# Two up-product chunks as products over halves of the rows, in a two-layer encoder on one core

## The chip, the core and the metric

The kernel runs on one core of a Trainium2 chip. The core's engines are TensorE (PE in the profile, with its weight loads as PEld), VectorE (DVE), ScalarE (ACT), GpSimd (POOL) and SyncE (SP), which here only issues transfers. The metric is device time in microseconds (us) of one execution. Each number is from runs on the chip or from the hardware profile of one execution.

## The reference

The program is a trunk of two encoder layers over 256 tokens of width 2048 (`D_MODEL`), in float32. Each layer is a norm, a token mixer and a residual add, then a norm, a gated MLP with a convolution of width 3 and a residual add. Layer 0 mixes with a bidirectional mLSTM, layer 1 with a bidirectional HGRN2. The change lies in the MLP of layer 0:

```python
D_FF = 5504
def conv_glu(hn, w_up, conv_w, conv_b, w_down):
    u = hn @ w_up
    a, v = jnp.split(u, 2, axis=-1)
    ...
    c = conv_b
    for j in range(CONV_W):
        c = c + ap[:, j:j + s] * conv_w[j]
    return (jax.nn.gelu(c, approximate=False) * v) @ w_down
```

## The kernel before, in words

**Products in two parts.** Every large product is made of float32r products. A weight piece `raw` is cast by ScalarE to `wh` (line 154), and VectorE subtracts that from `raw` to get the rest `wl` (line 155). The activations are split in the same way: `xt` holds, for each block of 128 features, 256 columns (tokens) of the leading part and 256 of the rest. One product of `wh` with all 512 columns (line 202) and one of `wl` with the first 256 (line 206) make up a 128x128 block of weights against all tokens.

**Chunks and pieces.** All weights go through one stream. `split_weights` (line 123) loads them in transfers of 1 MB, casts and subtracts them in pieces of 1024 columns, with three `raw` buffers and four each of `wh` and `wl`. `stream` (line 161) asks for pieces three ahead and walks over the chunks. An up-chunk (kind "fm", 256 output features) has sixteen blocks of input features (`nk`, index k) in four pieces. For each k it has two feature blocks f, gate (f = 0) and value (f = 1), each with its own PSUM bank `ps[f]`, and for each f the products "h" and "l". That is 64 products per chunk.

**Eviction.** At the end of a chunk `done_up` (line 842) empties the banks: `fm_scaled` has ScalarE copy columns 256 to 511 of a bank to `b` (line 231), VectorE add columns 0 to 255 (line 232) and multiply by the norm's factor (line 237). Then VectorE makes the convolution (lines 851 to 853), ScalarE the Gelu (line 854), VectorE the gating (line 855), and the result is split for the down-product (lines 857, 858).

**Banks.** The pool `psm` has four banks under the tag "mm". A chunk takes two of them (line 175), so one chunk can be evicted while the next one is multiplied.

**Order.** The program is written in the order of the loops, and a scheduler places the instructions on each engine's queue by its own simulated times. [...]

**The MLP's chunks.** `ffn` (loop at line 862) has two parts: 22 up-chunks and then their four down-chunks, and 21 up-chunks and their four down-chunks. In the trace the up-chunks of the first part of layer 0 follow each other every 11.09 us; their Gelu (line 854) starts at 548.30 us for i = 12, at 559.39 for i = 13 and at 570.49 for i = 14.

Of the kernel before, what the change touches and what calls it, by code (L numbers as in the profile page):

```python
# [8 lines left out]
F32 = mybir.dt.float32  # L9
# [3 lines left out]
ALU = mybir.AluOpType  # L13
PSUM = bass.MemoryType.PSUM

P = 128
T = 256
# [38 lines left out]
def trunk_kernel(ctx, tc, xT, x_d, fg_d, pp_d, cst_d, w_first, w_aq, w_ak, w_av, w_ao, w_aout,  # L56
                 w_bq, w_bv, w_bg, w_bout, w_up, w_down, out, mscr):
    nc = tc.nc
    act, dve, pool, pe = nc.scalar, nc.vector, nc.gpsimd, nc.tensor
# [3 lines left out]
    ev = ctx.enter_context(tc.tile_pool(name="ev", bufs=1))  # L63
    psm = ctx.enter_context(tc.tile_pool(name="psm", bufs=4, space=PSUM))
# [13 lines left out]
    def col(name, i):  # L78
        o = OFF[name] + i
        return pp[:, o:o + 1]  # L80
# [5 lines left out]
    class Side:  # L86
        def __init__(self):
            self.now, self.jobs = 0.0, []
# [25 lines left out]
    side = Side()  # L114


    class Chunk:
        def __init__(self, kind, src, nk, x, done, before=None, last=False, swap=()):
            self.last, self.swap = last, swap
            self.kind, self.src, self.nk, self.x, self.done, self.before = kind, src, nk, x, done, before  # L120
            self.width = {"fm": 256, "tm": 512, "first": 512 + P}[kind]

# [38 lines left out]
    def stream(chunks):  # L161
        pieces = split_weights(chunks)
        ready = []

        def fetch():
            p = next(pieces, None)
            if p is not None:
                ready.append(p)

        for _ in range(LOOK):  # L170
            fetch()
        for ch in chunks:
            if ch.before:
                ch.before()
            ps = [psm.tile([P, 512], F32, tag="mm", name="mm") for _ in range(3 if ch.kind == "first" else 2)]
            k = 0
            while k < ch.nk:
                fetch()
                wh, wl, n = ready.pop(0)
                if ch.last and k + sum(p[2] for p in ready) + n == ch.nk:  # L180
                    pieces_, k0 = [(wh, wl, n)] + ready, k
                    for t in range(2):
                        k = k0
                        for wh, wl, n in pieces_:
                            for kk in range(n):
                                x, c = ch.x(k), slice(kk * 512, (kk + 1) * 512)
                                xh, xl = x[:, t * P:(t + 1) * P], x[:, T + t * P:T + (t + 1) * P]
                                pe.matmul(ps[t], xh, wh[:, c], start=False, stop=False)
                                pe.matmul(ps[t], xh, wl[:, c], start=False, stop=False)
                                pe.matmul(ps[t], xl, wh[:, c], start=False, stop=k == ch.nk - 1)  # L190
                                k += 1
                        ch.half(ps[t], t)
                    return
                if ch.kind == "fm":
                    ops = [(kk, f, part) for kk in range(n) for f in range(2) for part in "hl"]
                    for i in ch.swap if k == 0 else ():
                        ops[2 * i + 1:2 * i + 3] = ops[2 * i + 2], ops[2 * i + 1]
                    for kk, f, part in ops:
                        x = ch.x(k + kk)
                        c = kk * ch.width + f * P  # L200
                        if part == "h":
                            pe.matmul(ps[f], wh[:, c:c + P], x, start=k + kk == 0, stop=False)  # L202
                            continue
                        if f:
                            side.tick(0.65)
                        pe.matmul(ps[f][:, 0:T], wl[:, c:c + P], x[:, 0:T], start=False, stop=k + kk == ch.nk - 1)  # L206
                    k += n
                    continue
                for kk in range(n):
                    x = ch.x(k)  # L210
                    st, sp = k == 0, k == ch.nk - 1
                    c = slice(kk * 512, (kk + 1) * 512)
                    for t in range(2):
                        xh, xl = x[:, t * P:(t + 1) * P], x[:, T + t * P:T + (t + 1) * P]
                        pe.matmul(ps[t], xh, wh[:, c], start=st, stop=False)  # L215
                        pe.matmul(ps[t], xh, wl[:, c], start=False, stop=False)  # L216
                        pe.matmul(ps[t], xl, wh[:, c], start=False, stop=sp)  # L217
                    if ch.kind == "first":
                        pe.matmul(ps[2], wh[:, 512:512 + P], x, start=st, stop=False)
                        pe.matmul(ps[2][:, 0:T], wl[:, 512:512 + P], x[:, 0:T], start=False, stop=sp)  # L220
                    side.tick(1.3)
                    k += 1
            ch.done(ps)

    def split(dst, src, gcol, pin=lambda ins: ins):
# [8 lines left out]
    def fm_scaled(ps, R, dst, scale=None):  # L234
        fm_sum(ps, dst)
        if scale is None:
            dve.tensor_tensor(dst, dst, R, ALU.mult)
        else:
            dve.scalar_tensor_tensor(dst, dst, scale, R, ALU.mult, ALU.mult)
# [144 lines left out]
    def project(wsrc, nk, x, norm):  # L384

        def done(c):
            def f_(ps):
                for t in range(2):
                    h = hm[:, t, 512 * c:512 * c + 512]
                    dve.tensor_tensor(h, h, ps[t], ALU.add)  # L390
                if norm is not None:
                    norm.add(c)
            return f_
        chunks = [Chunk("tm", wsrc(c), nk, x, done(c)) for c in range(4)]
        if isinstance(norm, FinalNorm):
            chunks[3].last, chunks[3].half = True, norm.half
        return chunks

    def slot(j, name, more=None):
        where = keep if j < KT else more  # L400
        return where.tile([P, 2 * T], F32R, tag=f"yt{j}", name=f"{name}{j}")
# [429 lines left out]
    def ffn(layer, norm, nxt):  # L831
        stack = ExitStack()
        box = {}
        chunks = []

        def begin():
            box["mp"] = stack.enter_context(tc.tile_pool(name="ff", bufs=1))
            box["mp"].tile([P, LEAD], F32, name="lead")
            if isinstance(nxt, FinalNorm):
                nxt.begin(box["mp"])  # L840

        def done_up(f, i, GT):
            def go(ps):
                mp, R = box["mp"], norm.R
                a = mp.tile([P, T], F32, tag="a", bufs=2, name="a")
                v = mp.tile([P, T], F32, tag="v", bufs=2, name="v")
                c = mp.tile([P, T], F32, tag="c", bufs=2, name="c")
                fm_scaled(ps[0], R, a)
                fm_scaled(ps[1], R, v)
                cw = [col("conv_w", (layer * 3 + w) * FT + f) for w in range(3)]  # L850
                dve.tensor_scalar(c, a, cw[1], col("conv_b", layer * FT + f), ALU.mult, ALU.add)
                dve.scalar_tensor_tensor(c[:, 1:T], a[:, 0:T - 1], cw[0], c[:, 1:T], ALU.mult, ALU.add)
                dve.scalar_tensor_tensor(c[:, 0:T - 1], a[:, 1:T], cw[2], c[:, 0:T - 1], ALU.mult, ALU.add)
                act.activation(c, c, AF.Gelu)
                dve.tensor_tensor(c, c, v, ALU.mult)
                g = slot(i, "g", mp)
                act.copy(g[:, 0:T], c)
                dve.tensor_tensor(g[:, T:2 * T], c, g[:, 0:T].bitcast(F32), ALU.subtract)
                GT.append(g)
            return go  # L860

        for part, (f0, nf) in enumerate(((0, FA), (FA, FB))):
            GT = []
            for i in range(nf):
                chunks.append(Chunk("fm", w_up[layer, f0 + i], KT, norm.x, done_up(f0 + i, i, GT),
                                    begin if f0 + i == 0 else None,
                                    swap=(1 + (layer == 0),) if part and i == 0 else ()))
            chunks += project(lambda c: w_down[layer, c][:, f0 * 512:(f0 + nf) * 512], nf,
                              lambda k, GT=GT: GT[k], nxt if part else None)
        return chunks, stack.close  # L870
# [7 lines left out]
    for i in range(39):  # L878
        o = i % 4 * QUAD
        pe.matmul(idle[o:o + QUAD, 0:120], ones[:, 0:QUAD], ones[:, 0:120], start=True, stop=True)  # L880
    n0, n1, n2, n3 = Norm("mix_g", 0), Norm("ffn_g", 0), Norm("mix_g", KT), Norm("ffn_g", KT)
    nf = FinalNorm()
    chunks = mlstm(n0, n1)
    c, close0 = ffn(0, n1, n2)
    chunks += c
    c = hgrn(n2, n3)
    b = c[0].before
# [6 lines left out]
    c, close1 = ffn(1, n3, nf)  # L894
    chunks += c
    stream(chunks)
    close1()

# [81 lines left out]
```

## Time and profile before

| | |
|---|---|
| time, median of 3 runs | 2419.44 us (2418.76 to 2421.82) |
| the profiled execution: time | 2421.37 us |
| the profiled execution: span of the core | 2419.6 us |
| granted TensorE clock, mean | 0.999 |
| PE busy | 2406.7 us, 99% of the span |
| products of line 202 (512 columns) | 3776, 1315.6 us busy |
| products of line 206 (256 columns) | 3776, 1048.8 us busy |
| VectorE, ScalarE busy | 1694.1 us (70%), 1221.1 us (50%) |

The time of the profiled execution lies 1.9 us above the median of the runs, and its span 1.8 us below its own time. In the profile's rows a line gives its line number in the kernel, the engine, the operation, output and inputs by name, the shapes, and how often it occurs; `128*32` ahead of the shapes stands for the rows and columns of the array that a product uses. Products overlap in the array, so the sum of their durations is more than the time they take; starts tell the pace.

### The profile page before, as it was taken

The numbers are of one execution on the slowest core, as the hardware profiler recorded it, in microseconds if no ns is written. First come the engines' busy times: TensorE is split into PE (matmuls) and PEld (weight loads), VectorE is DVE, ScalarE is ACT, GpSimd is POOL, SyncE is SP. The second block draws the span as 40 slices with busy tenths as digits, with TensorE's granted clock in tenths as the row PEclk, the third lists the DMA queues.
The fourth block names the chain that finished last, engine by engine and source line by source line (L and its number), as shares of the span: only waits on it lengthen the run. The fifth ranks groups of instructions, "written<-read, shape, count | busy, mean of one in ns | idle before, by whom it ended". The sixth has DMA issues, their size and how long they took to land.

```text
span 2419.6 us, 36956 instructions
## 1 busy us (share of the span) xinstructions
PE 2406.7 (99%) x14646; PEld 2060.3 (85%) x14646; DVE 1694.1 (70%) x2784; ACT 1221.1 (50%) x1879; POOL 161.7 (7%) x223
## 2 busy tenths in 40 slices
PE   9999999999999999999999999999999999999998
PEld 7888888888888888888888888888888888888887
DVE  7766656777645777656898989885777754677754
ACT  6655455444434445445555555555544443444443
POOL 0100000000000000001222222220000000000000
PEclk9999999999999999999999999999999999999999
DMA  8654555555555555555545554555555555555554
GB/s 290 200 182 162 186 176 189 190 188 189 181 196 201 188 187 189 192 185 183 173 173 175 175 175 167 168 185 190 183 191 190 192 188 195 194 190 192 192 188 142
DMA packets 66925, 451.90 MB, mean 187 GB/s; under 512 B 7600, under 2 KB 8368, under 8 KB 14144
## 3 DMA queue, kind: packets, MB, share of 16 engines
q1 hardware_dynamic: 64656, 442.92, 54.0%
q0 software_dynamic: 1232, 5.31, 0.9%
q8 instruction: 114, 1.87, 0.3%
q10 hardware_dynamic: 864, 1.32, 0.2%
q14 instruction: 59, 0.48, 0.1%
HBM read 447.35 MB, written 2.16 MB: 186 GB/s over the span
## 4 chain that ended last, share of the span: by engine, by line
PE 98%; DMA 1%; DVE 0%; issue 0%; ACT 0%; SPq 0%; POOLq 0%; POOL 0%; DVEq 0%
PE mm L202 36%; PE mm L206 18%; PE mm L215 13%; PE mm L216 13%; PE mm L217 13%; DMA gx<-in_xT 1%; PE pn L533 1%; PE py L763 1%; PE pd L713 0%; PE pz L288 0%; PE pa L713 0%; PE S L519 0%; PE pz L784 0%; PE pa L738 0%; PE pa L737 0%
## 5 line engine op out<-in xcount | busy, mean ns | idle before, releaser
L155 DVE TENSOR_TENSOR wl<-raw,wh 128x1024 fp32r<-128x1024 f32 (+1 forms) x848 | 1031.9, 1218 | 582.3 <-ACT wh L154 572.4
L202 PE MATMUL mm<-xt,wh 128*128 128x512 f32 x3776 | 1315.6, 394 | 0.0
L154 ACT CAST wh<-raw 128x1024 fp32r<-128x1024 f32 (+1 forms) x848 | 881.2, 1041 | 859.0 <-PE mm L217 400.9
L206 PE MATMUL mm<-xt,wl 128*128 128x256 f32 x3776 | 1048.8, 278 | 0.0
L202 PEld LDWEIGHTS mm<-xt,wh 128*128 128x128 f32 x3776 | 707.0, 188 | 160.7
L206 PEld LDWEIGHTS mm<-xt,wl 128*128 128x128 f32 x3776 | 710.0, 188 | 3.2 <-DVE wl L155 0.3
L217 PE MATMUL mm<-wh,g 128*128 128x512 f32 x674 | 262.8, 390 | 0.0
L215 PE MATMUL mm<-wh,g 128*128 128x512 f32 x674 | 262.5, 390 | 0.0
L216 PE MATMUL mm<-wl,g 128*128 128x512 f32 x674 | 262.3, 389 | 0.0
L215 PE MATMUL mm<-wh,xt 128*128 128x512 f32 x512 | 198.9, 393 | 2.9 <-ACT xt L226 2.1
L216 PE MATMUL mm<-wl,xt 128*128 128x512 f32 x512 | 198.5, 392 | 0.2 <-DVE wl L155 0.2
L217 PE MATMUL mm<-wh,xt 128*128 128x512 f32 x512 | 198.0, 391 | 0.0
L231 ACT COPY b<-mm 128x256 f32<-128x256 f32 x237 | 87.6, 369 | 166.6 <-PE mm L206 166.5
L217 PEld LDWEIGHTS mm<-wh,g 128*128 128x128 f32 x674 | 126.5, 188 | 26.5
L215 PEld LDWEIGHTS mm<-wh,g 128*128 128x128 f32 x674 | 126.5, 188 | 26.4
L216 PEld LDWEIGHTS mm<-wl,g 128*128 128x128 f32 x674 | 126.5, 188 | 25.8
L215 PEld LDWEIGHTS mm<-wh,xt 128*128 128x128 f32 x512 | 95.1, 188 | 23.2 <-ACT xt L226 3.3
L217 PEld LDWEIGHTS mm<-wh,xt 128*128 128x128 f32 x512 | 96.1, 188 | 20.0 <-DVE xt L227 0.4
L216 PEld LDWEIGHTS mm<-wl,xt 128*128 128x128 f32 x512 | 96.1, 188 | 19.9 <-DVE wl L155 1.2
L232 DVE TENSOR_TENSOR a<-mm,b 128x256 f32<-128x256 f32 x86 | 36.5, 424 | 52.2 <-ACT b L231 52.2
L705 DVE COPY kq<-QK 128x256 f32<-128x256 f32 x224 | 69.6, 335 | 0.0
L731 POOL TENSOR_TENSOR G<-G 128x384 f32<-128x384 f32 (+2 forms) x96 | 67.8, 706 | 6.3
(206 smaller groups left out, 1836.7 us busy)
## 6 DMA issues: line engine op xcount, KB each, us to landing
raw<-in_w_up SPq DMA_DIRECT2D x172, 1024.0 KB, 5.0
raw<-in_w_down SPq DMA_DIRECT2D x80, 1024.0 KB, 4.8
raw<-in_w_bq SPq DMA_DIRECT2D x48, 1024.0 KB, 5.0
raw<-in_w_ao SPq DMA_DIRECT2D x16, 1024.0 KB, 4.8
raw<-in_w_aout SPq DMA_DIRECT2D x16, 1024.0 KB, 4.7
raw<-in_w_bv SPq DMA_DIRECT2D x16, 1024.0 KB, 4.7
raw<-in_w_bg SPq DMA_DIRECT2D x16, 1024.0 KB, 4.7
raw<-in_w_bout SPq DMA_DIRECT2D x16, 1024.0 KB, 4.8
```

The lines of the kernel that those rows point to most:

```text
L154: pin(act.copy(wh[:, :m], r))
L155: pin(dve.tensor_tensor(wl[:, :m], r, wh[:, :m].bitcast(F32), ALU.subtract))
L202: pe.matmul(ps[f], wh[:, c:c + P], x, start=k + kk == 0, stop=False)
L206: pe.matmul(ps[f][:, 0:T], wl[:, c:c + P], x[:, 0:T], start=False, stop=k + kk == ch.nk - 1)
L215: pe.matmul(ps[t], xh, wh[:, c], start=st, stop=False)
L216: pe.matmul(ps[t], xh, wl[:, c], start=False, stop=False)
L217: pe.matmul(ps[t], xl, wh[:, c], start=False, stop=sp)
L231: act.copy(b, ps[:, T:2 * T])
L232: dve.tensor_tensor(dst, ps[:, 0:T], b, ALU.add)
L533: pe.matmul(pn[:, 0:258], w, v, start=(i == 0), stop=(i == len(parts) - 1))
L705: dve.tensor_copy(m[:, j].rearrange("k (m p j) -> k m p j", p=2, j=h), blocks(z, h, 0, T))
L731: pool.tensor_tensor(G2, G[:, 0:6 * n:2], G[:, 1:6 * n:2], ALU.mult)
```

## The change

The chunks i = 13 and i = 14 of the first part in layer 0 get `rows=64`. Such a chunk takes four banks rather than two. Each of its products becomes two, one over rows (partitions) 0 to 63 of weights and activations and one over rows 64 to 127, the first into bank `ps[f]`, the second into `ps[2 + f]`. The columns stay as they were. At the end of the chunk ScalarE copies each of the two lower banks whole to a buffer of 512 columns, VectorE adds it to the upper bank in place, and `done_up` goes on as before. The buffer shares the tag "jk", of which there is one. All other chunks keep their code.

```diff
-        def __init__(self, kind, src, nk, x, done, before=None, last=False, swap=()):
-            self.last, self.swap = last, swap
+        def __init__(self, kind, src, nk, x, done, before=None, last=False, swap=(), rows=P):
+            self.last, self.swap, self.rows = last, swap, rows
...
-            ps = [psm.tile([P, 512], F32, tag="mm", name="mm") for _ in range(3 if ch.kind == "first" else 2)]
+            ps = [psm.tile([P, 512], F32, tag="mm", name="mm") for _ in range(3 if ch.kind == "first" else 4 if ch.rows < P else 2)]
...
+                if ch.rows < P:
+                    for kk in range(n):
+                        x = ch.x(k + kk)
+                        for f in range(2):
+                            c = kk * ch.width + f * P
+                            for w, m in ((wh, 2 * T), (wl, T)):
+                                for r in range(2):
+                                    o = slice(r * 64, r * 64 + 64)
+                                    pe.matmul(ps[2 * r + f][:, 0:m], w[o, c:c + P], x[o, 0:m],
+                                              start=m > T and k + kk == 0, stop=m == T and k + kk == ch.nk - 1)
+                        side.tick(0.65)
+                    k += n
+                    continue
...
+            if ch.rows < P:
+                for f in range(2):
+                    b = ev.tile([P, 512], F32, tag="jk", bufs=1, name="half")
+                    act.copy(b, ps[2 + f])
+                    dve.tensor_tensor(ps[f], ps[f], b, ALU.add)
             ch.done(ps)
...
-                                    swap=(1 + (layer == 0),) if part and i == 0 else ()))
+                                    swap=(1 + (layer == 0),) if part and i == 0 else (),
+                                    rows={13: 64, 14: 64}.get(i, P) if not layer and not part else P))
```

## The prediction

> **What bounds the kernel now.** I read the busy shares and the chain that ended last first, to see which engine sets the end.
>
> ```profile
> PE 2406.7 (99%) x14646; PEld 2060.3 (85%) x14646; DVE 1694.1 (70%) x2784; ACT 1221.1 (50%) x1879; POOL 161.7 (7%) x223
> ...
> PE 98%; DMA 1%; DVE 0%; issue 0%; ACT 0%; SPq 0%; POOLq 0%; POOL 0%; DVEq 0%
> ```
>
> PE is the path from end to end, so a stage costs what PE needs for it. The Gelu rows in ScalarE's timeline (line 854) put the thirteenth of the first layer's up-chunks (i = 12) at 548.30 us, so the matmuls of i = 13 and 14 lie at about 544.05 to 566.24. The windows view gives this stretch, and PE's timeline its grain:
>
> ```profile
> 544.05:555.14 11.09, 11.09 (x67) 9.69 (x65) 8.11 (x13) 5.47 (x9) 0.00 (x0) 1.00 0.58 191
> 555.14:566.24 11.10, 11.10 (x67) 9.71 (x66) 8.10 (x13) 5.49 (x9) 0.00 (x0) 1.00 0.55 190
> ```
> ```profile
> 544.04 0.39 PE L202 MATMUL mm<-xt,wh 128*128 128x512 f32 x1
> 544.27 0.27 PE L206 MATMUL mm<-xt,wl 128*128 128x256 f32 x1
> 544.39 0.40 PE L202 MATMUL mm<-xt,wh 128*128 128x512 f32 x1
> ```
>
> A chunk takes 11.09 us, with no gap. Starts, not durations, are the price: a 512-column product holds PE for 0.23 us and a 256-column one for 0.116 (544.27 to 544.39), together 0.347; 32 such pairs are the 11.1 us. Durations (394, 278 ns) add about 0.16 of fill that overlaps the next product. So the two chunks are 22.19 us, DVE has 3 us of slack in each, ScalarE 5.6.
>
> **The products.** Each of the 128 products of the two chunks becomes two, over rows 0 to 63 and 64 to 127, with the same columns: 256 products of 231 or 116 ns. Does a product over half the rows cost half? The nearest rows say no: the 64-row transpose of 64 columns takes 247 ns, the 128-row ones of 128 columns 272, and the 25 ns between them are 64 columns at the rate of the up-products (116 ns for 256). Columns set the time. One after another the 256 would therefore take 44.4 us, 22.2 more than now. They can only stay near 22 us if the two halves, which use different rows of the array, run at the same time. No row of the trace has two row groups at once. The nearest one has four column groups at once:
>
> ```profile
> L880 PEld LDWEIGHTS idle<-ones x78: 110/177/178, 1.1 to 4.5; 128*32 128x32 f32 x78
> L880 PE MATMUL idle<-ones x78: 266/407/408, 1.1 to 4.6; 128*32 128x120 f32 x78
> ```
>
> 78 products start within 3.5 us, 45 ns apart, though each lasts 407: they start in bunches of four, 7 ns apart, with about 200 ns from bunch to bunch. The hgrn products (line 713) do the same with their weight loads:
>
> ```profile
> 1165.78 0.80 PEld L713 LDWEIGHTS pd<-kq 128*32 128x32 f32 x79
> ```
>
> 79 loads of 108 ns each fit in 0.80 us. I take it that row groups overlap as column groups do. [...]
>
> **The order.** Overlap needs the two halves next to each other, since products start in order. The order of the changed program (as built) shows where the scheduler put them. In i = 13 the second feature block's banks come free late, so for the first six k its upper halves (6 of 512 columns, 6 of 256) are issued in one run and its lower halves in another: 6 × 0.347 = 2.08 us of each without a partner. In i = 14, 25 upper-half products of the first block (13 × 0.231 + 12 × 0.116 = 4.40 us) come before the first lower half, which overlaps the last of them (-0.23); later a run of five upper halves (0.93, less 0.23) leaves the lower rows idle again. After that the lower rows are busy throughout. Walking through this order with 231 and 116 ns, each product starting when its predecessor has started and its own rows are free, gives 13.20 + 15.87 = 29.07 us (28.95 when the chunks overlap at their border). That is 6.8 over 22.19: 2.1 from i = 13 and 4.7 from i = 14.
>
> **The banks.** A chunk of halves takes all four banks. Three borders count:
> - 12 to 13: the first block's two banks were emptied a chunk ago. The second block's wait for the evictions of i = 12, which end 0.7 and 3.1 us into the chunk (lines 232, below); PE comes to them after 2.0 and 4.1 us. Nothing.
> - 13 to 14: the first product waits until ScalarE has copied the first 512-column half out. From the start of the last product of that bank: 274 ns until it ends, 37 ns to ScalarE (as b at 543.89 after a product that ended at 543.86), 587 ns for the copy (the 128x512 copy of line 749), about 50 back: 0.95 us, of which PE has 0.464 in the second block's last two pairs. Stall 0.49 us. Behind the copy in ScalarE's queue stands the cast of i = 14's fourth weight piece, needed 4 us later. The other banks wait for the VectorE adds (680 ns by line 390) and for the evictions of i = 13 behind them, done about 4.7 us into the chunk; PE comes to them after 6 us or more.
> - 14 to 15: the same copy, 0.49 us; the weights for i = 15 were cast during i = 14.
>
> ```profile
> 544.30 0.42 DVE L232 TENSOR_TENSOR a<-mm,b 128x256 f32<-128x256 f32 x1 [0.59 <-ACT b L231]
> 544.76 0.43 DVE L237 TENSOR_TENSOR a<-a,R 128x256 f32<-128x256 f32 x1
> 545.26 1.23 DVE L155 TENSOR_TENSOR wl<-raw,wh 128x1024 fp32r<-128x1024 f32 x1
> 546.40 0.41 DVE L851 TENSOR_SCALAR c<-a,pp 128x256 f32<-128x256 f32 x1
> 546.73 0.42 DVE L232 TENSOR_TENSOR v<-mm,b 128x256 f32<-128x256 f32 x1
> ```
>
> **Copies and adds.** Four of 0.587 on ScalarE, four of 0.68 on VectorE: 1.2 and 1.4 us per chunk, under the slack of 5.6 and 3. If that cover failed, a weight piece would come late by at most one cast or subtraction, 1.05 or 1.23 us, at each border. No DMA moves: the orders of SP and POOL are unchanged. Going into and out of the halves costs about 0.1 us once (start to start is 205 ns rather than 112 where 128-column products give way to column groups at 1165.27); the way out lies in a stall.
>
> **The sum.** 6.8 + 1.0 + 0.1 = +7.9 us. On the profiled execution (2421.37 us, span 2419.6) that is 2429.3; on the median of the runs, 1.9 lower, 2427.3. Bounds within this case: -0.8 if the halves run at the shortest spacing of the trace (226 ns between the products of lines 215 to 217, 112 for 256 columns: 28.95 × 338/347), a further -1.0 if nothing is left of the two stalls; +2.5 if ScalarE or VectorE is in the middle of a cast or subtraction at both borders. So 2425.5 to 2430.
>
> **Rivals.**
> 1. *Weight loads become the bound.* Halves double the loads. Transposes that reload 128 columns each start 109 ns apart (four in 0.60 us with 0.27 for one), so a load may take 110 ns of a shared path. Then a paired round, four products and four loads, needs 231 + 220 ns instead of 347, and the walk gives 33.8 us: +11.6 + 1.1 = +12.8, 2432.2. It decides as soon as loads to the two row groups exclude each other. For it: 85% busy PEld and no row-group loads to look at; against it: the 79 loads in 0.80 us. [...]
> 2. *The halves run one after the other.* +22.2 and stalls of 0.15 each (PE then has 0.81 us of work beside the copy): +22.6, 2442. For it: no row group pair in the trace; against it: the column groups.
> 3. *Faster: a product's time goes by its rows.* If each half took half as long and they overlapped, 28.95 would be 14.5, and with 1.1 of stalls the stretch would be 6.6 us shorter: 2412.8. It decides once a pair costs under 254 ns of its row group's time (21.1 of 28.95 × 347). The 247 and 272 ns speak against it.
> 4. *The change does not do what it says*, since the scheduler separates the halves: that is partly so, and is in the sum.
>
> **Chances.** Overlap with hidden loads 0.53, loads as bound (or a mixture) 0.22, serial 0.16, faster 0.03, under 4.8 us of loss for causes that I do not see 0.06. 0.2% (4.8 us) is about what a measurement of this kernel can tell from no change. The likeliest case gives 2427.3. The range has to reach to the serial case: 2425.5 to 2443. Slower 0.91, within 0.2% 0.06, faster 0.03.
>
> **What would show it.** In the profile after: 128 products of 64*128 with 512 columns and 128 with 256; in the stretch from 544.05, upper and lower halves starting a few ns apart with 0.35 us per two pairs if they overlap (0.45 by rival 1, 0.69 by rival 2); i = 13 about 13.2 us long and i = 14 about 15.9; a run of 25 upper halves without partner at its head; two PE gaps near 0.5 us, released by ScalarE's 512-column copy; everything after shifted by a constant. I am wrong on the mechanism if the two windows sum to over 32 or under 27 us, and on the stalls if PE's gaps there exceed 3 us.

## The result, and the profile after

The changed kernel takes 2428.32 us (median of 4 runs, 2427.36 to 2431.92) against 2419.14 for the kernel before on the same chip: a ratio of 1.0037, 95% interval 1.0025 to 1.0049, so 9.2 us longer (6 to 12 by the interval). The profiled execution is the longest of the four, 2431.92 us with a span of 2430.1.

PE is still the path from end to end (first the busy times on the page, then the chain):

```profile
PE 2417.8 (99%) x14774; PEld 2070.2 (85%) x14774; DVE 1697.4 (70%) x2788; ACT 1223.3 (50%) x1883; POOL 161.7 (7%) x223
...
PE 98%; DMA 1%; ACT 1%; issue 0%; DVE 0%; POOLq 0%; POOL 0%; SPq 0%; ACTq 0%; DVEq 0%
```

PE has 128 products more, VectorE 4 and ScalarE 4. In the numbering of this kernel the half products stand on line 202, the full ones on 215 and 219, ScalarE's copy on 239. PE's groups inside the stretch:

```profile
L202 PE MATMUL mm<-xt,wh 64*128 64x512 f32 x128 | 31.1, 430 | 0.3 <-ACT half L239 0.3
L202 PE MATMUL mm<-xt,wl 64*128 64x256 f32 x128 | 26.9, 295 | 0.0
```

A product over 64 rows lasts as long as one over 128: the medians are 388 and 277 ns, against 394 and 278 on average before (the means in the two rows, 430 and 295, are raised by a stretch of lower clock, below). Two run at once. PE's timeline at the first of them (`x2`: two that start together):

```profile
542.92 0.28 PE L219 MATMUL mm<-xt,wl 128*128 128x256 f32 x1
543.13 0.50 PE L202 MATMUL mm<-xt,wh 64*128 64x512 f32 x2
543.47 0.28 PE L202 MATMUL mm<-xt,wl 64*128 64x256 f32 x2
543.59 0.40 PE L202 MATMUL mm<-xt,wh 64*128 64x512 f32 x2
```

The first two start 4 ns apart, and further on a round of four half products takes 347 ns, as one pair of full products did.

The stretch runs from 543.13 us to the first full product at 575.28: 32.15 us, against 22.19. The chain over its borders:

```profile
554.96 0.93 PE mm L202 x11
555.90 0.02 issue
555.92 0.59 ACT half L239
556.51 0.04 issue
556.56 18.01 PE mm L202 x110
574.57 0.02 issue
574.59 0.02 ACTq L239
574.61 0.04 issue
574.64 0.59 ACT half L239
575.24 0.04 issue
575.28 0.50 PE mm L215
```

At both borders PE waits for the same thing: one 0.59-us copy by ScalarE. Chunk 13 lasts from 543.13 to 556.07. The next start comes 0.602 us after a 256-column product, which holds PE for 0.116: a stall of 0.49. Chunk 14 then runs to 574.74, and the second stall is 0.660 - 0.116 = 0.54. In the windows view (busy us and instructions of PE, PEld, DVE, ACT, POOL, then the granted clock, DMA share and GB/s) chunk 14 shows something that no step of the prediction had:

```profile
557.00:559.00 2.00, 2.00 (x13) 1.72 (x12) 1.75 (x3) 1.21 (x3) 0.00 (x0) 1.00 0.10 37
559.00:561.00 2.00, 2.00 (x9) 1.73 (x8) 1.97 (x6) 0.37 (x1) 0.00 (x0) 0.59 0.68 152
561.00:563.00 2.00, 2.00 (x11) 1.74 (x10) 1.39 (x4) 0.47 (x2) 0.00 (x0) 0.50 0.89 373
563.00:565.00 2.00, 2.00 (x10) 1.80 (x11) 0.43 (x1) 0.35 (x1) 0.00 (x0) 0.50 0.00 0
565.00:567.00 2.00, 2.00 (x20) 1.76 (x17) 0.00 (x0) 0.00 (x0) 0.00 (x0) 0.70 0.00 0
```

PE is busy all the time, but the granted clock is 0.50 from 559.36 to 566.19. At half pace these 6.83 us cost 3.41. Without them chunk 14 would be 14.77 us, and the stretch 28.74.

So the added time of this execution is 1.0 us of stalls, 5.5 us in which one half of the rows had no partner (12.94 + 14.77 against 22.19, 0.1 of start included), 3.4 us of half clock, and, after the stretch, a slower pace: the Gelu starts of chunks 15 to 18 are 11.3 us apart rather than 11.1. The last is seen in the summaries of the Gelu line, of before and then of after (first and last start of four consecutive chunks):

```profile
L854 ACT ACTIVATE c<-c x4: 417/418/419, 581.6 to 614.9; 128x256 f32<-128x256 f32 x4
```
```profile
L872 ACT ACTIVATE c<-c x4: 418/420/422, 590.8 to 624.7; 128x256 f32<-128x256 f32 x4
```

It comes to 0.21 us per chunk (a pair of full products takes 353.3 ns rather than 346.7). The seven up-chunks that are left take 79.11 us, to the first down-product at 654.39, against 77.65 before: 1.5 us more, 0.1 of which is PE's start after the stall. When the down-chunks begin it is gone.

These terms add up to 11.4 us, and the spans of the two profiles differ by 10.5. The rest lies ahead of the changed code: this execution reached chunk 13 0.9 us earlier than that of before. In all the profiles of this text the first up-product starts between 396.1 and 398.9 us, while the time from the first down-product to the end is 1775.4 to 1775.9 us in each. What a kernel does from chunk 13 to the down-chunks therefore shows the change more sharply than its whole time.

### The profile page after: what moved, and what is told of

It reads as the page before. It is cut to its first block, busy times and chain, and to the rows that moved or that the text cites. A ratio compares the mean times of both kernels' runs of the same rounds, so it can differ in the third digit from the quotient of the medians.

```text
span 2430.1 us, 37225 instructions
## 1 busy us (share of the span) xinstructions
PE 2417.8 (99%) x14774; PEld 2070.2 (85%) x14774; DVE 1697.4 (70%) x2788; ACT 1223.3 (50%) x1883; POOL 161.7 (7%) x223
## 4 chain that ended last, share of the span: by engine, by line
PE 98%; DMA 1%; ACT 1%; issue 0%; DVE 0%; POOLq 0%; POOL 0%; SPq 0%; ACTq 0%; DVEq 0%
PE mm L215 35%; PE mm L219 18%; PE mm L228 13%; PE mm L230 13%; PE mm L229 13%; PE mm L202 1%; PE pn L551 1%; PE py L781 1%; PE pd L731 0%; DMA gx<-in_xT 0%; PE pz L306 0%; PE pa L731 0%; DMA raw<-in_w_first 0%; PE S L537 0%; ACT wh L154 0%
## 5 line engine op out<-in xcount | busy, mean ns | idle before, releaser
L215 PE MATMUL mm<-xt,wh 128*128 128x512 f32 x3712 | 1294.9, 395 | 0.4 <-ACT half L239 0.4
L219 PE MATMUL mm<-xt,wl 128*128 128x256 f32 x3712 | 1031.7, 279 | 0.4 <-DVE wl L155 0.4
L215 PEld LDWEIGHTS mm<-xt,wh 128*128 128x128 f32 x3712 | 695.0, 188 | 159.0 <-ACT half L239 0.7
L219 PEld LDWEIGHTS mm<-xt,wl 128*128 128x128 f32 x3712 | 698.2, 188 | 4.2 <-DVE wl L155 1.2
```

## The experiments

The theory to be tested: side by side, halves cost what full rows cost. The loss comes from the banks, which make PE wait and make the scheduler separate the halves; the lower clock and the slower pace are set off by what the halves leave of the array's use. The rivals: that halves cost by themselves, or that the copies and adds do.

**The changed kernel again.** No edit.

> The changed kernel once more, to see whether the half clock that its first profile shows (6.8 us at a granted clock of 0.5, from 559.4 us on) comes in every execution. If it hangs on the runs of half-row products, the profile shows it again or not by where those runs fall in the clock's own windows: with it about 2430 to 2432 us, without it 2427 to 2428. The two parts without the half clock, the lost partners (5.5 us) and the two stalls (1.0), are expected in every execution; also the pace of 0.354 us per pair instead of 0.347 in the up-chunks that follow (1.5 us).

Measured: 2427.67 us (2425.95 to 2428.85) against 2419.67 before, ratio 1.0032 [1.0020, 1.0043]. In this profile the clock in the stretch stays at 1.00 (chunk 13, then chunk 14):

```profile
543.56:556.40 12.84, 12.84 (x129) 11.95 (x128) 8.38 (x13) 5.38 (x9) 0.00 (x0) 1.00 0.48 158
556.99:572.59 15.60, 15.22 (x128) 13.10 (x129) 9.67 (x16) 6.62 (x11) 0.00 (x0) 1.00 0.42 138
```

The stretch takes 29.03 us, +6.84: chunks of 12.94 (0.1 for the start included) and 15.06, stalls of 0.48 and 0.54. The first window above ends 0.1 us before its chunk does, and the second holds the second stall too. The pace after the stretch is soon the old one (Gelu starts 599.3 to 621.5 over two chunks), though the slow pace had been expected in every execution. Neither the half clock nor the slow pace is. What is in both is the rest: +6.6 in the first profile (28.74) and +6.8 in this one.

**Lower halves in banks of their own.** The two lower banks come from a pair that lies idle in this stage.

```diff
-            ps = [psm.tile([P, 512], F32, tag="mm", name="mm") for _ in range(3 if ch.kind == "first" else 4 if ch.rows < P else 2)]
+            ps = [psm.tile([P, 512], F32, tag="mm", name="mm") for _ in range(3 if ch.kind == "first" else 2)]
+            if ch.rows < P:
+                ps += [aux("lo") for _ in range(2)]
```

> The lower halves get two banks of the pool that the mixers use, which lies idle in this stage, so no bank is waited for; as built, all 128 pairs then stand side by side. Theory (the halves overlap fully, the loss is lost partners and stalls from bank waits): the two chunks take 22.2 to 22.6 us instead of 28.7 to 32.2, no half clock, total 2419 to 2420 us, ratio to the kernel before 1.000 within 0.001. Rival (loads or the array make a pair of halves dearer than one full product): over 0.35 us per pair, 26 us or more for the two chunks, total 2423 us or more.

Measured: 2421.73 us (2420.91 to 2423.55), ratio 1.0009 [1.0000, 1.0018]. PE's timeline at the start names the two halves `mm` and `lo`; the second fence is the whole stretch:

```profile
542.42 0.49 PE L204 MATMUL mm<-xt,wh 64*128 64x512 f32 x1
542.43 0.49 PE L204 MATMUL lo<-xt,wh 64*128 64x512 f32 x1
542.76 0.28 PE L204 MATMUL mm<-xt,wl 64*128 64x256 f32 x1
542.76 0.27 PE L204 MATMUL lo<-xt,wl 64*128 64x256 f32 x1
```
```profile
542.42:565.22 22.80, 22.80 (x257) 21.91 (x256) 17.61 (x28) 11.65 (x19) 0.00 (x0) 1.00 0.48 162
```

The 256 half products take 22.80 us, against 22.19 for the 128 full ones, with no stall and no half clock; the copies and adds, two of each behind the stretch, hold no product up. The stretch is 0.2 us above the 22.6 that the theory allowed, and far below the rival's 26. The 0.6 are 0.2 of start and way out (0.333 us and 0.203 where 0.231 and 0.116 are usual) and 0.4 of slow pace; in the chunks that follow, the slow pace adds 1.5. So the halves with their copies and adds bring 0.6 of the stretch's 6.84 us. What this kernel has not got is the shared banks.

**Full rows in four banks.** Chunks 13 and 14 with full products, even k into one pair of banks and odd k into the other, with the same copies and adds.

```diff
+                        r = (k + kk) % 2
...
-                                for r in range(2):
-                                    o = slice(r * 64, r * 64 + 64)
-                                    pe.matmul(ps[2 * r + f][:, 0:m], w[o, c:c + P], x[o, 0:m],
-                                              start=m > T and k + kk == 0, stop=m == T and k + kk == ch.nk - 1)
+                                pe.matmul(ps[2 * r + f][:, 0:m], w[:, c:c + P], x[:, 0:m],
+                                          start=m > T and k + kk == r, stop=m == T and k + kk == ch.nk - 2 + r)
```

> Full-row products as before the change, but even k go to two banks and odd k to two others, with the same four copies and adds: the bank waits of the change without half rows. Theory: two PE gaps of about 0.5 us, 22.2 + 1.0 us for the two chunks, no half clock, total 2420 to 2420.5 us, and 2421.5 to 2422 if the slower pace of the following chunks (0.354 us per pair) comes from the gaps. Rival (the half clock is set off by the gaps and not by the half rows): 6.8 us at half clock, 3.4 us more.

Measured: 2423.03 us (2421.76 to 2423.66), ratio 1.0013 [1.0004, 1.0022]. The stretch takes 23.70 us, +1.5: stalls of 0.49 and 0.67 behind the same copy, 0.1 where PE starts again, and 0.3 of slow pace, from the middle of chunk 13 on. The clock stays at 1.00:

```profile
544.52:568.23 23.71, 22.88 (x131) 19.43 (x129) 16.51 (x28) 12.31 (x20) 0.00 (x0) 1.00 0.44 152
```

The bank waits by themselves cost 1.2 us; the rest of the changed kernel's 6.84 needs the halves. The whole time is above the 2420 to 2422 expected: from chunk 13 to the down-chunks the profile has +1.8 us, and the medians are 3.4 apart. The other 1.6 are not in the chunks that the edit touches or behind them; where they come from is open.

**Runs of sixteen.** Banks of their own again, but for each weight piece sixteen upper products and then sixteen lower ones, in an order that is kept.

```diff
+                    pin = tc.keep_in_program_order
+                    for r in range(2):
+                        o = slice(r * 64, r * 64 + 64)
+                        for kk in range(n):
...
+                                    pin(pe.matmul(ps[2 * r + f][:, 0:m], w[o, c:c + P], x[o, 0:m], ...
```

> As own_banks, but with an order written out: sixteen products of the upper rows, then sixteen of the lower rows, piece by piece. No bank waits, no gaps; the halves are too far apart to pair. If products start strictly in order, the two chunks take 42.7 us (+20.5, 2440 us); if a row group runs about four products ahead of the other, 34.0 us (+11.8, 2431 us). On the half clock: if half-used rows set it off, it shows here though PE has no gap, and each 6.8 us of it add 3.4; if gaps set it off, it does not.

Measured: 2435.89 us (2434.83 to 2436.30), ratio 1.0067 [1.0053, 1.0080]; the stretch is 36.21 us, with PE busy throughout and the clock at 1.00:

```profile
542.12:578.33 36.21, 36.21 (x258) 32.02 (x257) 17.78 (x28) 12.05 (x19) 0.00 (x0) 1.00 0.37 128
```

So the order alone, without any bank wait, brings a loss. The size lies between one after the other (44.4) and side by side (22.8), and between the two that were expected (42.7 and 34.0). PE's timeline at a change from a run of upper halves (`mm`) to one of lower halves (`lo`) shows why it is below a strict order:

```profile
548.65 0.28 PE L205 MATMUL mm<-xt,wl 64*128 64x256 f32 x1
548.77 0.40 PE L205 MATMUL mm<-xt,wh 64*128 64x512 f32 x1
548.77 0.50 PE L205 MATMUL lo<-xt,wh 64*128 64x512 f32 x1
549.01 0.28 PE L205 MATMUL mm<-xt,wl 64*128 64x256 f32 x1
549.12 0.28 PE L205 MATMUL lo<-xt,wl 64*128 64x256 f32 x1
549.13 0.40 PE L205 MATMUL mm<-xt,wh 64*128 64x512 f32 x1
549.24 0.39 PE L205 MATMUL lo<-xt,wh 64*128 64x512 f32 x1
549.36 0.27 PE L205 MATMUL mm<-xt,wl 64*128 64x256 f32 x1
```

In program order all `mm` of a run come before the first `lo`. Yet three of them, at 549.01, 549.13 and 549.36, start after `lo` has begun. A product whose rows are free starts while up to three earlier ones wait for theirs: at each of the fifteen changes of run in the trace, the first product of the new run starts ahead of exactly three of the old one. That is the expectation's case of 34.0 us. In addition every run opens slowly, with 0.34 us from its first start to its second where 0.231 is usual; sixteen times 0.105 make it 35.7, and 0.5 us are left, of the size of the slow pace.

The clock did not fall here, which by the expectation spoke for the stalls as its cause. The twenty chunks and the part rows below say otherwise.

**Twenty chunks.** The change, the full rows in four banks, and the banks of their own, each for chunks 1 to 20 instead of two of them; and the banks of their own for chunks 20 and 21, the last before the down-chunks.

```diff
-                                    rows={13: 64, 14: 64}.get(i, P) if not layer and not part else P))
+                                    rows=64 if 1 <= i <= 20 and not layer and not part else P))
```

> The change's form for i = 1 to 20 instead of 13 and 14: as built, nineteen chunks have the order of i = 14 (25 upper halves without partner at the head). Each is expected to take 14.8 + 0.5 + 0.1 = 15.3 to 15.4 us instead of 11.1: about +82 us in all (2502 us) without half clock. On the half clock: if it takes a PE gap and a run of half rows in the same window of the clock's control (the first profile of the change had both in the 3.4 us before it, the second profile had the run alone in one window), a window fits by chance once in some five or six borders, so 2 to 6 spells of 6.8 us are expected here, 3.4 us each. If the one spell had nothing to do with the change, none or one.

> full_rows_four_banks for i = 1 to 20: gaps as in twenty_chunks, but all rows of the array in use. The gaps and restarts cost 0.6 us per border, with the slower pace (0.353 us per pair, 0.2 us per chunk) after each of them 0.8: +12 to +17 us, 2432 to 2437. No half clock if the half rows are needed for it; 2 to 6 spells if the gaps suffice.

> own_banks for i = 1 to 20: all 1280 pairs of halves side by side, no bank waits. If a pair costs what a full product costs, the twenty chunks take 221.9 us plus 0.6 for going in and out, 2420 us in all; if the slower pace holds throughout, 4 us more, 2424. If a pair cost 5 ns more than a full product, 6 us more. Under 2418 us would mean that pairs are cheaper than full products. No half clock.

> own_banks with i = 20 and 21, the last up-chunks of the part, in place of 13 and 14. own_banks lost 0.6 us in its two chunks and 1.3 us in the seven up-chunks after them, which ran at 0.353 us per pair until the down-chunks. If that slower pace is something that a restart leaves behind and that lasts until the next change of kind, it has no chunks to act on here: 22.8 us for the two chunks and +0.6 us in all, 2420.3 us. If the 1.3 us belong to the two chunks themselves (late weights or evictions), they are lost here too: 2421.6 us.

| kernel | time, us (range) | ratio to before, 95% interval | stretch, us, beside 221.9 (20 chunks) or 22.19 (2) |
|---|---|---|---|
| the change, 20 chunks | 2522.87 (2522.80 to 2522.94) | 1.0423 [1.0402, 1.0444] | 325.90, +104.0 |
| full rows in four banks, 20 chunks | 2441.31 (2440.95 to 2441.66) | 1.0086 [1.0066, 1.0107] | 243.95, +22.1 |
| banks of their own, 20 chunks | 2424.89 (2424.55 to 2425.95) | 1.0020 [1.0010, 1.0031] | 227.64, +5.7 |
| banks of their own, last 2 | 2420.54 (2419.40 to 2422.56) | 1.0003 [0.9994, 1.0013] | 22.80, +0.6 |

The change does not become better by being used more. Its 104 us are four spells of half clock (13.7; 2 to 6 spells had been expected), and 4.5 per chunk of the rest, a little more than the 4.2 to 4.3 expected: stall and lost partners, with each chunk inside like chunk 14, not like the cheaper chunk 13. The full rows cost more than expected, 1.1 us per chunk: 0.7 to 0.8 of it is the stall, which is longer here than the 0.49 of two chunks. Yet with a stall at each border they have no spell, so stalls alone do not bring the clock down:

```profile
408.98:652.93 243.95, 232.09 (x1286) 195.88 (x1284) 184.25 (x299) 129.52 (x201) 0.00 (x0) 1.00 0.49 171
```

The banks of their own lose 0.27 us per chunk, mostly the slow pace (0.21). And with the last two chunks, after which no up-chunk can run at that pace, the loss by the medians is 1.1 us rather than 2.1. The intervals overlap, but the profiles say the same more sharply: from the first half product to the down-chunks it is +0.6 us here and +2.2 with chunks 13 and 14, so the slow pace in the chunks behind is the difference.

The four spells tell when the clock drops. They begin at 456.9, 538.8, 620.7 and 654.8 us: 81.9 and 34.1 apart, 12 and 5 times the 6.83 us of a spell. Half of that, 3.41 us, is the step: the second profile of the changed kernel has a spell of that length at its head (15.50 to 18.91), one of 37.5 us, 11 such steps, follows below, and the full clock ahead of the first profile's spell and behind it is recorded for 552.96 and 1860.26 us, 162 and 545 steps. So the clock seems to be decided once per window of 3.41 us. For each window of the stretch I added up the time that products take (231 or 116 ns at full clock), a half product counted as half. The five windows just ahead of a spell, four here and the one of the profile after, have a share of 0.40 to 0.41 of the window. The next lowest at full clock, which no spell follows, have 0.41 and 0.43, the lowest in the runs of sixteen 0.57, and the lowest in the twenty chunks of full rows 0.72. Moving the edges of the windows by 0.02 us changes a share by up to 0.005, so these windows do not place the border more closely than at about 0.41. Where a window held the stall and otherwise a run of upper halves alone, it fell below; where the stall lay across two windows, or the halves were side by side in part of it, as in the second profile (0.58), it did not. Here are the window ahead of the first spell, the two of the spell, and the one after it:

```profile
453.50:456.90 3.40, 3.02 (x18) 2.35 (x17) 2.30 (x3) 2.29 (x4) 0.00 (x0) 0.99 0.43 178
456.90:460.30 3.40, 3.40 (x16) 2.94 (x15) 2.85 (x8) 0.79 (x2) 0.00 (x0) 0.50 0.78 243
460.30:463.70 3.40, 3.40 (x19) 3.10 (x17) 0.85 (x2) 0.41 (x1) 0.00 (x0) 0.50 0.16 65
463.70:467.10 3.40, 3.40 (x36) 2.97 (x34) 1.03 (x1) 1.08 (x2) 0.00 (x0) 1.00 0.00 0
```

**Part of the rows alone.** That share was found afterwards, so it was put to a test without any stall: chunks 13 and 14 as in the kernel before, but each product over the first 32, 48, 56 or 64 rows. The products over the other rows, and with them a part of the two chunks' sums, are left out.

```diff
+                                pe.matmul(ps[f][:, 0:m], w[0:ch.rows, c:c + P], x[0:ch.rows, 0:m],
+                                          start=m > T and k + kk == 0, stop=m == T and k + kk == ch.nk - 1)
```

> Chunks i = 13 and 14 in the kernel before's form (two banks, no copies or adds, no waits), but each product over rows 0 to 31 only; the other three quarters of the contraction are left out. PE has no gap there, and a quarter of the array is in use. Share theory (the clock is halved after a 3.41-us window in which the rows in use, weighted by their time, are under about 0.41 of the array): 0.25 in every window of the stretch, so at least one spell of 6.83 us (+3.4), and up to the whole rest of the stretch at half clock (about 17 us of full-speed work, +17): 2423 to 2437. Gap theory (it takes an idle gap and a part-row run in one window): no spell, 2419.4 as before. In both, columns set a product's time, so 32 pairs stay at 0.347 us each at full clock; if rows set it, the stretch would fall to a quarter, 2403.

> As the run before it, with rows 0 to 47 (five eighths of the contraction left out). Share theory: 48/128 = 0.375, below the lowest share that left the clock alone (0.409) and below the five that set a spell off (0.398 to 0.407): spell or spells, at least +3.4, 2423 to 2437. Gap theory: none, 2419.4. If not rows but row groups of 32 or 64 count, 48 rows count as 0.5: none, 2419.4.

> As the run before it, with rows 0 to 55: 56/128 = 0.4375. Share theory: above the highest share that set a spell off (0.407) and above the lowest two that did not (0.409, 0.432): no spell, 2419.4. Gap theory: none either. A spell here would put the bound above 0.44 and speak against the share theory's bound, though not against the share.

> As the run before it, with rows 0 to 63: a share of 0.5 for 22 us without a gap. Share theory and gap theory: no spell, 2419.4, stretch 22.19 us. A theory by which a long run of half rows alone halves the clock (the longest so far without a gap was about 2.8 us): a spell, +3.4 or more. If a product's time went by its rows, the stretch would be 11 us and the time 2408.

| rows | share | time, us (range) | ratio to before, 95% interval | stretch, us | at half clock, us |
|---|---|---|---|---|---|
| 0 to 31 | 0.25 | 2439.71 (2437.96 to 2441.45) | 1.0085 [1.0056, 1.0114] | 38.83 | 41.0 |
| 0 to 47 | 0.375 | 2437.97 (2437.41 to 2438.53) | 1.0078 [1.0049, 1.0107] | 37.34 | 37.5 |
| 0 to 55 | 0.4375 | 2422.90 (2421.07 to 2423.51) | 1.0010 [0.9999, 1.0021] | 22.39 | none |
| 0 to 63 | 0.5 | 2421.69 (2421.03 to 2423.54) | 1.0010 [0.9999, 1.0022] | 22.39 | none |

The stretch with 48 rows ahead of the spell and in it, and the whole stretch with 56 and with 64 rows:

```profile
543.95:548.60 4.65, 4.65 (x28) 4.07 (x28) 4.37 (x9) 2.83 (x5) 0.00 (x0) 1.00 0.51 150
548.60:581.30 32.70, 32.70 (x105) 27.27 (x103) 12.30 (x19) 8.38 (x13) 0.00 (x0) 0.50 0.34 120
```
```profile
543.93:566.32 22.39, 22.39 (x130) 19.38 (x129) 16.27 (x26) 10.96 (x17) 0.00 (x0) 1.00 0.56 190
```
```profile
543.01:565.40 22.39, 22.39 (x129) 19.38 (x129) 16.27 (x26) 10.96 (x17) 0.00 (x0) 1.00 0.57 189
```

PE has no gap in any of them. With 48 rows the clock falls to 0.50 after one full window and stays there for eleven; with 56 it never falls. Both spells, with 32 and with 48 rows, last 5 us longer than the part rows, which puts both times above the 2437 us that had been the upper end expected. So no stall is needed: what counts is how much of the array's rows is in use, and the border lies between 0.375 and 0.4375, where the windows of the changed kernel had put it (about 0.41). All these products use 128 columns; whether it is the rows alone or the part of the array in use was not separated. Rows 56 and 64 also show that at full clock a product's time does not go by its rows: 22.39 us, 0.2 of it start and way out. By the medians they cost 3.5 and 2.3 us all the same, with intervals that just reach a ratio of 1; in both profiles it is 1.8 us from chunk 13 to the down-chunks, most of it the slow pace behind the stretch (353.3 ns per pair).

No kernel of these comes out ahead of the kernel before.

## Why the prediction was right, and where it was off

The mechanism held, and the predicted 2427.3 us is 1.0 below the first median and 0.4 below the second. That it comes so close is in part luck: one term was 1.1 to 1.4 us too large, and two costs that some executions have were not in the sum. Step by step:

- **Columns, not rows, set the time.** Right: 22.39 us for chunks with 56 or 64 rows, where by rows it would have been about 11. The row that this rested on was weaker than it was read: the 247 ns are the middle of a pair of products that took 223 and 271.
- **The halves overlap.** Right, and as the column groups had it: 4 ns between starts, 347 ns per round, 22.80 us for both chunks where every half has its partner. One after the other would be 44.4 (256 products at 231 or 116 ns). So two row groups give 44.4 / 22.8 = 1.95 times. Ahead of the runs no row showed it; that row groups do what column groups do was my assumption.
- **Weight loads (rival 1).** They do not bound: a round with four loads takes 347 ns. At the 109 ns between the transposes' loads, one after the other, an estimate for the loads alone is 436. (The terms of this rival add up to +12.7 rather than +12.8 us, and the 254 ns of rival 3 come out as 253; nothing hangs on either.)
- **Lost partners.** The one term that was mis-sized: 6.8 us predicted, 5.4 and 5.7 measured (12.94 + 14.77 and 12.94 + 15.06, less 22.19 and 0.1 of start; 13.20 + 15.87 had been forecast). The step "products start in order", on which the walk rests, failed. The rows of before show it for full products alone (544.04, 544.27, 544.39). In the runs of sixteen it holds within a row group, not between two: a lower half starts ahead of three upper ones, at 548.77 us ahead of those at 549.01, 549.13 and 549.36. The same walk with three earlier products left to wait gives 12.72 + 14.80, and with 0.1 us more wherever a row group starts after a wait, as the runs of sixteen have it, 12.93 + 15.01.
- **The banks.** Right in place and size: no gap from 12 to 13 (the timeline at 542.92 and 543.13), then 0.49 and 0.54 us against 0.49 forecast for each, by the 0.59-us copy (the 50 ns back to PE, for which no row was given, are 40 in the chain above). What the sum could not contain is that such a stall, next to a run of halves, can take the clock along (0.50 for 6.83 us in the first profile).
- **Copies and adds.** Hidden, as said: in banks of their own the stretch has no gap, and its 0.6 us are accounted for without them.
- **Going in.** 0.1 us, as said.
- **A constant shift behind it.** Wrong in some executions: 1.4 us of slow pace follow in the first profile. The profile of the second set has 0.3 behind a stretch of +6.84, yet the set's median is +8.0. If most of its executions ran at the slow pace, which is not shown, the sum of +7.9 met that by two errors of opposite sign: 1.1 us too much for the lost partners, nothing for the pace.
- **The half clock.** Not foreseen. It puts the stretch of the first profile at 32.15 us, just over the 32 that I had named as the sign of a wrong mechanism; without it the stretch is 28.7. A bound on a sum of windows needs the granted clock beside it.
- **Rival 4**, the halves separated by the scheduler, makes most of the loss. Of the 6.6 and 6.8 us that the two profiles have beside the half clock, 5.4 and 5.7 come from it, 1.0 from the waits and 0.1 from the start.

What is not settled: what makes pairs of full products take 353.3 rather than 346.7 ns after some stretches of halves and not after others (the changed kernel has both, and the full-row chunks in four banks run in part at the slow one), and the last microsecond or so between profiles and medians. Executions differ before the first changed chunk already: in the profiles that change nothing ahead of chunk 13, the Gelu of chunk 11 lies between 2.3 us ahead of that in the profile of before and 0.55 behind it.

## What to carry to other kernels

Splitting a product that already uses all rows into row groups gained nothing here: two halves side by side took about the time of one whole (22.80 us for the two chunks, against 22.19), and every half without a partner took that time again (231 or 116 ns). What decides is therefore the order on PE's queue and the banks behind it: look at where a scheduler puts the two halves, and give them banks that no eviction holds. And where products over few rows run alone, read the granted clock of the stretch, even if PE is shown as busy without a gap (0.50 over 32.70 us of PE work with 48 rows).

## What the runs showed of the hardware that was not expected

- In the runs of sixteen, products of different row groups overtake each other by up to three places: `lo` at 548.77 us ahead of three `mm` that come earlier in the program, and the same at all fifteen changes of run. A product that waited for its rows did not hold those behind it that use other rows; PE's starts kept the order of the program within a row group alone.
- The clock went by the share of the rows in use, with PE busy throughout: at 0.25 and 0.375 for 22 us of work it fell to 0.50 for 41.0 and 37.5 us, at 0.4375 and 0.5 it stayed at 1.00. The spells seen last whole steps of 3.41 us (3.41, 6.83, 37.5 and 41.0 are 1, 2, 11 and 12 of them), and so do the distances between those of the twenty chunks (81.9 and 34.1 us are 24 and 10). PE's busy time does not tell the four runs apart, since PE has no gap in any of them; the share of the rows does.
- A pair of full products has two paces, 346.7 and 353.3 ns. In the first profile the slower one lasts to the end of the up-chunks, at 654.39 us, and is worth 0.21 us per chunk; in the second it soon gives way to the other.
